# A two-layer streaming encoder step: the MLPs' down projections by seven block products instead of eight, PSUM as four two-bank tiles

## The chip, the cores and the metric

The kernel runs on one core of a Trainium2 chip. The metric is the device time of one execution in microseconds (us), compared by the median over runs. About 0.2% (5 us) is what a measurement of this kernel can tell from no change.

Engine names follow the profile: PE multiplies matrices (PEld is its loading of the stationary operand), DVE is the vector engine, ACT the scalar engine, POOL the GpSimd engine, SP issues most DMA transfers. PSUM is the accumulator memory that PE writes, eight banks of 512 float32 columns on 128 partitions; SBUF is the working memory.

## The reference

One inference step of a trunk with two layers, 1024 features, on 1024 prompt frames and 32 sample frames. Layer 0 mixes tokens with a gated linear recurrence (HGRN2), layer 1 with a gated depthwise convolution of width 3. Both are followed by the same kind of MLP, and a last norm ends the step:

```python
def trunk(x, ...):
    h = x
    for i in range(DEPTH):
        a = rmsnorm(h, norm_mix[i])
        if i % N_MIXERS == 0:
            y, s = hgrn2_mixer(a, ...)
        else:
            y, s = short_conv_mixer(a, ...)
        h = h + y
        m = rmsnorm(h, norm_mlp[i])
        h = h + jnp.square(jax.nn.relu(m @ w_up[i])) @ w_down[i]
    return rmsnorm(h, norm_final), ...
```

`w_up` is 1024 x 4096 and `w_down` 4096 x 1024, so each of the MLP's two products has 1024 x 4096 weights over 1056 tokens. All is float32.

## The kernel before, in words

**Layout.** Activations lie transposed: features on the 128 partitions, the 1056 tokens (prompt and sample together) along the columns. A tensor of 1024 features is eight tiles of 128 x 1056. Tokens are taken in three groups of 384, 384 and 288 (`GROUPS`, L28), each of which fits one PSUM bank.

**Precision.** A float32 operand is used as two float32r parts: a rounded upper part and the remainder. `wsplit` (L94) loads a 512 x 256 block of weights by SP's DMA into `raw`, ACT rounds it into `whi` (L91) and DVE subtracts it into `wlo` (L92). A product is three matmuls (`mm3`, L104): low weights by upper activations, upper by low, upper by upper, accumulated in one bank.

**Order.** The kernel is written as a plain sequence; a planner of the framework orders each engine's instructions ahead of time by their place in the program and by when it thinks their operands and buffers are free. That order is fixed when the kernel runs; each engine takes its queue in order, and semaphores hold an instruction until its operands are there. Weight blocks rotate through four pairs of `whi` and `wlo` buffers and three `raw`, so the loads and splits of the next blocks are interleaved with the work on the current ones. PSUM is two pools of single-bank tiles, three `pj` and five `rc`; `bank()` (L171) takes them in turn. Eighteen long buffers of 128 x 1056 (the pool `fp`, tag `ft`) hold the residual stream `hT` (eight of them) and, in the MLP, the activations.

**The MLP** (`mlp`, L668) goes over the 4096 inner features in eight chunks of 512. Up: for each of the chunk's four column blocks and each token group, 8 row tiles x 3 matmuls into a bank, then DVE applies relu and the norm's factor (L688), ACT squares (L689) and rounds to `uh` (L690), DVE subtracts to `ul` (L691). Down: for each of the eight output blocks and each group, 4 row tiles x 3 matmuls, then DVE adds the bank into `hT` (L698). After the last chunk of the first MLP, `fin0` adds the row's squares into the next norm's sum (`Norm.add`, L623: a square on ACT, a sum on POOL) and splits the row for the convolution (`split`, L175: ACT, then DVE at L182). In the last chunk of the second MLP the down part goes group by group (`FGROUPS`, L29), and the final norm of a finished group (`fin1`) runs among the next group's matmuls. `Norm.scale` (L632) sums the squares over the partitions with three matmuls and works out 1/rms on DVE; the first evictions behind it wait for that factor.

The weights are laid out on the host (`_lay`): `_grid` makes each 512 x 256 block one contiguous piece, four tiles of 128 rows by 256 columns.

Of the kernel before, what the change touches and what calls it, by code (L numbers as in the profile page):

```python
# [8 lines left out]
F32 = mybir.dt.float32  # L9
# [14 lines left out]
FC = 512  # L24
NFC = FF // FC
# [4 lines left out]
# columns of the short vectors  # L30
# [4 lines left out]
def trunk_kernel(  # L35
# [24 lines left out]
    pj = ctx.enter_context(tc.tile_pool(name="pj", bufs=3, space=PSUM))  # L60
    rc = ctx.enter_context(tc.tile_pool(name="rc", bufs=5, space=PSUM))
# [19 lines left out]
    vec = cp.tile([P, NV], F32, name="vec")  # L81

# [41 lines left out]

    def rsqrt(v, y, t):
        """y = 1/sqrt(v) for v > 0: first guess from the exponent bits, three Newton steps."""
# [7 lines left out]
    def tok_rsqrt(pool, accs, n, mid=None):  # L134
        """accs, each [128, n]: squares, still to be summed -> 1/rms per token, [128 tokens, blocks]"""
        nb = -(-n // P)
        ps = pjt()
# [18 lines left out]
    def tok_spread(y, n):  # L156
        """per-token values [128 tokens, blocks] -> the same on every partition, PSUM [128, n]"""
        out = []
        for g0 in range(0, n, 512):
            ps = pjt()  # L160
# [7 lines left out]

    banks = [0]

    def bank():  # L171
        banks[0] += 1
        return pjt() if banks[0] % 8 in (0, 3, 6) else rct()
# [10 lines left out]
    # =============== layer 0, HGRN2 mixer ===============  # L184
# [18 lines left out]
    # masks and the zeroed tiles whose unwritten parts stay zero  # L203
# [9 lines left out]
    # the sample tokens stand twice on the partitions: their values come in two summands (v_sample)  # L213
# [14 lines left out]
    def lower_bounds():  # L228
        """lower bound of the forget gate: first row of the softmax over the two rows"""
# [32 lines left out]
    def gates(H):  # L262
        """decays within blocks of 32, taken from the middle of the block"""
# [22 lines left out]
        # products of whole-block decays, per chunk of four blocks  # L286
# [35 lines left out]
    def carry(H):  # L322
# [6 lines left out]
        # keys decayed to the end, queries from the start, of their half (or quarter) chunk  # L329
# [36 lines left out]
    def o_turn(H, src, nt, nch, col):  # L366
        """normed o back to features on partitions, gained and gated in place of the gate"""
# [8 lines left out]
    def scores(H, half):  # L376
        """within the chunks: decayed keys against queries, masked, and the keys turned"""
# [131 lines left out]
    for pr in range(HEADS // 2):  # L509
# [57 lines left out]
        # the recurrence, step by step between the products of the remaining projections  # L567
# [18 lines left out]
    hp_cm.__exit__(None, None, None)  # L586

    # =============== shared by the rest ===============
    mp = ctx.enter_context(tc.tile_pool(name="mp", bufs=1, reuse_waits="tile"))
    def mm_block(ps, n, c0, wt, j, srcs, kk0=0):  # L590
# [9 lines left out]
    def mm_rows(pss, wt, j, srcs, mid=None):  # L600
        """one block of 128 columns, all token groups, row tile by row tile: uses up the operands in turn"""
# [14 lines left out]
    class Norm:  # L616
        """sum of squares of hT over the features, collected as the rows of hT get final"""
# [14 lines left out]
        def scale(self):  # L632
            v = mp.tile([P, NTOK], F32, tag="sq", name="nv")
            for g in range(3):
                sl, n = gsl(g)
                ps = bank()
# [6 lines left out]
    def out_proj(W, first):  # L643
        """hT += W^T applied to the split activations; ends with the split of the next ones"""
        nrm = Norm()
        for m2 in range(4):
            wt = wload(W, m2)
            for j in range(2):
# [4 lines left out]
                pss = [bank() for g in range(3)]  # L653
# [13 lines left out]

    def mlp(layer, nrm, on_final, last):  # L668
        Wu, Wd = wg_up[layer], wg_down[layer]
        for c in range(NFC):  # L670
            uh = [fp.tile([P, NTOK], F32R, tag="ft", name=f"uh{j}") for j in range(4)]
            ul = [fp.tile([P, NTOK], F32R, tag="ft", name=f"ul{j}") for j in range(4)]
            for m2 in range(2):
                wt = wload(Wu, 2 * c + m2)
                for j in range(2):
                    m = 2 * m2 + j
                    first = c == m == 0
                    pss = [bank() for g in range(3)]
                    if first:
                        mm_rows(pss, wt, j, xsrc, nrm.scale)  # L680
                    for g in range(3):
                        sl, n = gsl(g)
                        ps = pss[g]
                        if not first:
                            mm_block(ps, n, sl.start, wt, j, xsrc)
                        r = nrm.r
                        t = mp.tile([P, 384], F32, tag="t", name="t", bufs=3)
                        nc.vector.scalar_tensor_tensor(t[:, :n], ps[:, :n], 0.0, r[:, sl], op0=ALU.max, op1=ALU.mult)  # L688
                        nc.scalar.activation(t[:, :n], t[:, :n], AF.Square)  # L689
                        nc.scalar.copy(uh[m][:, sl], t[:, :n])  # L690
                        nc.vector.tensor_tensor(ul[m][:, sl], t[:, :n], uh[m][:, sl].bitcast(F32), op=ALU.subtract)  # L691
            usrc = list(zip(uh, ul))

            def down(wt, m, j, c0, n):
                sl = slice(c0, c0 + n)
                ps = bank()
                mm_block(ps, n, sl.start, wt, j, usrc)
                nc.vector.tensor_tensor(hT[m][:, sl], hT[m][:, sl], ps[:, :n], op=ALU.add)  # L698

            dw = lambda m2: [wsplit(Wd[m2, c])]  # L700
            if c == NFC - 1 and last:
                wts = [dw(m2) for m2 in range(4)]
                for g in range(3):
                    for m in range(KT):
                        down(wts[m // 2], m, m % 2, *FGROUPS[g])
                        on_final(g, m)
            else:
                for m2 in range(4):
                    wt = dw(m2)
                    for j in range(2):  # L710
                        for g in range(3):
                            down(wt, 2 * m2 + j, j, *GROUPS[g])
# [192 lines left out]
```

## Time and profile before

| | |
|---|---|
| median of 3 runs | 2498.1 us (2497.3 to 2500.84) |
| span of the profiled execution, first to last instruction | 2495.9 us |
| median less that span | 2.2 us |
| busy PE, DVE, ACT, POOL | 99%, 46%, 24%, 6% of the span |
| mean granted clock of PE | 0.998 |

The span is that of one profiled execution; no other time is given for that execution. A busy share counts the time in which an engine has an instruction running. A row of a group of instructions gives line, engine, operation, output<-inputs, shape and count; after the bar the busy time in us and the mean of one in ns, then how long the engine was idle just before them and what ended that. A row of the timeline gives the start in us, the duration in us, then the instruction; in square brackets the idle time before it and what ended it. Matmuls overlap: each shows its whole latency, so the distance from one start to the next, not the duration, is what one costs. The table of stretches has one row per stretch of the span: length, then busy time of PE, PEld, DVE, ACT and POOL with instruction counts, the granted clock, the DMA engines' share and GB/s.

### The profile page before, as it was taken

Reading aid. Unit: us, or ns where it says so; the run is one execution under the profiler, and the core shown is the slowest. Engines: PE = TensorE matmul, PEld = TensorE weight load, DVE = VectorE, ACT = ScalarE, POOL = GpSimd, SP = SyncE. Lnnn points to the kernel's source line nnn. Section 1 sums busy time; section 2 is a strip of 40 time slices with the busy share of each in tenths; the row PEclk is TensorE's granted clock in tenths of the full one; section 3 lists DMA queues with packets and bytes.
Section 4 is the critical chain, followed back from the end, with each engine's and each line's share of the span. In section 5 each row is a group of like instructions: output and inputs, shape, how many; then the busy total and the mean of one; then the engine's idle time right before and its main releaser. Section 6 shows DMA issues by size and latency. Waiting matters only on the chain.

```text
span 2495.9 us, 36430 instructions
## 1 busy us (share of the span) xinstructions
PE 2474.1 (99%) x15852; PEld 2445.1 (98%) x15852; DVE 1160.3 (46%) x2023; ACT 589.9 (24%) x1020; POOL 159.2 (6%) x328
## 2 busy tenths in 40 slices
PE   8999999999999999999999999999999999999998
PEld 8999999999999999999999999999999999999997
DVE  8775757554533333333336533335533333333335
ACT  5121212133221221221223111123221221221224
POOL 2110101012000000000002000002000000000003
PEclk9999999999999999999999999999999999999999
DMA  4111010121111111111111111111111111111101
GB/s 148 38 32 44 28 48 22 54 106 51 43 43 51 43 43 51 46 39 51 51 35 51 50 35 51 52 34 51 51 35 51 51 34 51 52 36 50 51 26 70
DMA packets 35743, 121.81 MB, mean 49 GB/s; under 512 B 4336, under 2 KB 7552, under 8 KB 35584
## 3 DMA queue, kind: packets, MB, share of 16 engines
q1 hardware_dynamic: 33632, 113.58, 14.0%
q0 software_dynamic: 1952, 5.92, 0.7%
q8 instruction: 124, 2.03, 0.3%
q14 instruction: 35, 0.29, 0.0%
HBM read 114.09 MB, written 5.39 MB: 48 GB/s over the span
## 4 chain that ended last, share of the span: by engine, by line
PE 98%; DVE 1%; ACT 0%; DMA 0%; issue 0%; DVEq 0%; SPq 0%; ACTq 0%
PE rc L105 17%; PE rc L106 16%; PE rc L107 16%; PE pj L105 13%; PE pj L106 13%; PE pj L107 13%; PE v L490 1%; PE v L491 1%; PE v L492 1%; PE aps L383 1%; PE aps L388 1%; PE ops L425 1%; PE ups L400 1%; PE ops L424 1%; PE aps L386 0%; PE kps L393 0%
## 5 line engine op out<-in xcount | busy, mean ns | idle before, releaser
L105 PE MATMUL rc<-xh,wlo 128*128 128x384 f32 (+1 forms) x1600 | 518.9, 325 | 0.0
L106 PE MATMUL rc<-xl,whi 128*128 128x384 f32 (+1 forms) x1600 | 517.2, 323 | 0.0
L107 PE MATMUL rc<-xh,whi 128*128 128x384 f32 (+1 forms) x1600 | 516.7, 323 | 0.0
L105 PE MATMUL pj<-xh,wlo 128*128 128x288 f32 (+1 forms) x1472 | 480.5, 327 | 7.0 <-ACT xh L181 7.0
L106 PE MATMUL pj<-xl,whi 128*128 128x288 f32 (+1 forms) x1472 | 475.2, 323 | 1.9 <-DVE xl L179 1.9
L107 PE MATMUL pj<-xh,whi 128*128 128x288 f32 (+1 forms) x1472 | 474.5, 322 | 0.0
L91 ACT CAST whi<-raw 128x1024 fp32r<-128x1024 f32 (+1 forms) x201 | 209.9, 1046 | 950.5 <-PE rc L107 646.1
L105 PE MATMUL rc<-uh,wlo 128*128 128x288 f32 (+3 forms) x960 | 310.7, 324 | 0.0
L107 PE MATMUL rc<-uh,whi 128*128 128x288 f32 (+3 forms) x960 | 310.0, 323 | 0.0
L106 PE MATMUL rc<-ul,whi 128*128 128x288 f32 (+3 forms) x960 | 310.0, 323 | 0.0
L105 PEld LDWEIGHTS rc<-xh,wlo 128*128 128x128 f32 x1600 | 300.6, 188 | 0.4 <-ACT xh L181 0.2
L106 PEld LDWEIGHTS rc<-xl,whi 128*128 128x128 f32 x1600 | 300.8, 188 | 0.2
L107 PEld LDWEIGHTS rc<-xh,whi 128*128 128x128 f32 x1600 | 300.9, 188 | 0.0
L92 DVE TENSOR_TENSOR wlo<-raw,whi 128x1024 fp32r<-128x1024 f32 (+1 forms) x201 | 244.5, 1219 | 92.7 <-ACT whi L91 92.0
L105 PEld LDWEIGHTS pj<-xh,wlo 128*128 128x128 f32 x1472 | 276.5, 188 | 8.7 <-ACT xh L181 7.0
L106 PEld LDWEIGHTS pj<-xl,whi 128*128 128x128 f32 x1472 | 276.7, 188 | 2.3 <-DVE xl L179 2.3
L107 PEld LDWEIGHTS pj<-xh,whi 128*128 128x128 f32 x1472 | 276.6, 188 | 0.0
L698 DVE TENSOR_TENSOR hT<-hT,rc 128x288 f32<-128x288 f32 (+3 forms) x240 | 124.6, 520 | 251.8 <-PE rc L107 251.7
L689 ACT ACTIVATE t<-t 128x384 f32<-128x384 f32 (+1 forms) x192 | 95.4, 499 | 442.1 <-DVE t L688 440.3
L105 PE MATMUL pj<-uh,wlo 128*128 128x384 f32 (+3 forms) x576 | 186.2, 323 | 0.0
L106 PE MATMUL pj<-ul,whi 128*128 128x384 f32 (+3 forms) x576 | 185.9, 323 | 0.0
L107 PE MATMUL pj<-uh,whi 128*128 128x384 f32 (+3 forms) x576 | 185.7, 322 | 0.0
(214 smaller groups left out, 2916.4 us busy)
## 6 DMA issues: line engine op xcount, KB each, us to landing
raw<-in_wg_up_dram SPq DMA_DIRECT2D x64, 512.0 KB, 3.8
raw<-in_wg_down_dram SPq DMA_DIRECT2D x64, 512.0 KB, 3.2
raw<-in_wg_in_hgrn_dram SPq DMA_DIRECT2D x31, 512.0 KB, 4.0
raw<-in_wg_cu_conv_dram SPq DMA_DIRECT2D x16, 512.0 KB, 3.3
xk<-in_x_t_dram SPq DMA_DIRECT2D x8, 528.0 KB, 8.5
hT<-in_x_t_dram POOLq DMA_DIRECT2D x8, 528.0 KB, 7.2
raw<-in_wg_out_hgrn_dram SPq DMA_DIRECT2D x8, 512.0 KB, 3.9
raw<-in_wg_b_conv_dram SPq DMA_DIRECT2D x8, 512.0 KB, 3.3
```

Source lines behind the costliest of these rows:

```text
L91: nc.scalar.copy(hi, raw)
L92: nc.vector.tensor_tensor(lo, raw, hi.bitcast(F32), op=ALU.subtract)
L105: nc.tensor.matmul(ps, wlo, ah, start=start, stop=False)
L106: nc.tensor.matmul(ps, whi, al, start=False, stop=False)
L107: nc.tensor.matmul(ps, whi, ah, start=False, stop=stop)
L383: nc.tensor.matmul(o, H.K[:, sl], H.F[:, sl], start=True, stop=True)
L388: nc.tensor.matmul(o[0:64, 64:128], kl[:, 64:128], ql[:, 64:128], start=True, stop=True)
L400: nc.tensor.matmul(ups[:, ci * P : (ci + 1) * P], H.kT[half][:, ci], H.V[:, 4 * half + ci], start=True, stop=True)
L424: nc.tensor.matmul(o, H.C[:, c * P : (c + 1) * P], prev, start=True, stop=False)
L425: nc.tensor.matmul(o, at[half][:, ci], H.V[:, c], start=(c == 0), stop=True)
L689: nc.scalar.activation(t[:, :n], t[:, :n], AF.Square)
L698: nc.vector.tensor_tensor(hT[m][:, sl], hT[m][:, sl], ps[:, :n], op=ALU.add)
```

## The change

**Products.** Each MLP's inner features are taken in 16 chunks of 256 instead of 8 of 512. The down product of such a chunk, for each half of the 1024 output features, is cut into 2 x 2 blocks: weights by 128 inner features and 256 output features (two column tiles `p` of 128 to a block), activations by 128 inner features and half of the tokens (528). The block product is formed by seven products of sums of blocks (a form of Strassen's scheme with the sums nested as S1 to S4, T3, T4, Q1, Q2) where the plain form has eight. `STEPS` gives their order and the PSUM tile (`a`, `b` or `c`) each accumulates in: some products add to a tile whose earlier partial sum has already been read out, because that sum is needed in two output blocks. A product is three matmul passes over two token quarters of 264 columns, one per bank of a two-bank tile, and each product is followed by an eviction of 528 columns into `hT`.

**Evictions.** Those of steps 1 to 5 are DVE additions from PSUM. Those of steps 0 and 6 are copies by ACT into one of four `st` tiles and additions by POOL; in the last chunk of the first MLP (`final`) they are DVE additions too.

**Sums of weights** (`wsums`): a block's upper part and remainder are made for three of the four tiles as stored; then POOL forms four sums in place in `raw`, and ACT and DVE split those into a second pair of `whi` and `wlo` buffers. **Sums of activations** (`xsums`): seven operands, each a rounded part by ACT and a remainder by DVE, and four sums by DVE in place.

**Up part.** Two column blocks a chunk. The first two token groups share a two-bank tile and are evicted by one DVE instruction of 768 columns; relu, norm factor and square stay in float32 in the long buffers, the split now belongs to `xsums`.

**Order.** A chunk's up part is emitted, then the down part of the chunk before, then the sums of the chunk's activations. In the second MLP the last two chunks keep the plain product with the final norm among it; their activations are split into the operand tiles `xh`, `xl` that the up part has then done with.

**PSUM.** After the recurrence the two pools are closed, and one pool of four two-bank tiles takes their place. Every block of three groups in the rest of the kernel takes two such tiles (`trio`), and so do the norm's three matmuls; single uses take one (`newps`).

The host's layout of `w_down` changes with it (`_blocks`): the four tiles of a piece are the four blocks.

```diff
+    pb = ctx.enter_context(tc.tile_pool(name="pb", bufs=4, space=PSUM, reuse_waits="tile"))
+    def pt():
+        return pb.tile([P, 2, 512], F32, tag="pb", name="pb")
+    def trio():
+        a, b = pt(), pt()
+        return a, [a[:, 0], a[:, 1], b[:, 0]]
...
+    WAT = {"A11": (0, 0), "A12": (0, 1), "A22": (0, 2), "S2": (1, 0), "S4": (1, 1), "S1": (1, 2), "S3": (1, 3)}
+    STEPS = (("a", "A11", "B11", True), ("b", "S1", "Q1", True), ("a", "S2", "Q2", False), ("b", "S4", "B22", False),
+             ("a", "S3", "T3", False), ("c", "A12", "B21", True), ("a", "A22", "T4", False))
+    def wsums(src):
+        raw, hi, lo = wtiles()
+        hi2 = ws.tile([P, 4, 256], F32R, tag="whi", name="whi")
+        lo2 = ws.tile([P, 4, 256], F32R, tag="wlo", name="wlo")
+        nc.sync.dma_start(out=raw, in_=src)
+        nc.scalar.copy(hi[:, :3], raw[:, :3])
+        nc.vector.tensor_tensor(lo[:, :3], raw[:, :3], hi[:, :3].bitcast(F32), op=ALU.subtract)
+        for d, o in ((2, 3), (3, 0), (0, 2), (1, 0)):
+            nc.gpsimd.tensor_tensor(raw[:, d], raw[:, d], raw[:, o], op=ALU.add)
+        nc.scalar.copy(hi2, raw)
+        nc.vector.tensor_tensor(lo2, raw, hi2.bitcast(F32), op=ALU.subtract)
...
+    def xsums(u0, u1):
+        b11, b12, b21, b22 = u0[:, :HALF], u0[:, HALF:], u1[:, :HALF], u1[:, HALF:]
...
+            t = fp.tile([P, 2, HALF], F32R, tag="ft", name=f)
+            h, l = t[:, 0], t[:, 1]
...
+                nc.scalar.copy(h, src)
+                nc.vector.tensor_tensor(l, src, h.bitcast(F32), op=ALU.subtract)
...
+        part("B11", b11)
+        part("B22", b22)
+        add(b22, b12, b22, ALU.subtract)
+        add(b12, b11, b12, ALU.subtract)
+        add(b11, b22, b11, ALU.subtract)
+        part("Q1", b12)
+        part("Q2", b11)
+        part("T3", b22, True)
+        part("B21", b21)
+        add(b21, b11, b21, ALU.add)
+        part("T4", b21, True)
...
     def mlp(layer, nrm, on_final, last):
...
+                nc.vector.scalar_tensor_tensor(two(u), a[:, :, :384], 0.0, two(r), op0=ALU.max, op1=ALU.mult)
+                sq(u[:, :768])
+                nc.vector.scalar_tensor_tensor(u[:, 768:], pss[2][:, :288], 0.0, r[:, 768:], op0=ALU.max, op1=ALU.mult)
+                sq(u[:, 768:])
...
+        def down(c, final=False):
+            x = X.pop(c)
+            for b in range(2):
+                w = wsums(Wd[c, b])
+                ps = [{}, {}]
+                for i, (bank, f, g, start) in enumerate(STEPS):
+                    for p in range(2):
+                        if start:
+                            ps[p][bank] = pt()
+                        t = ps[p][bank]
+                        (hi, lo), (xhi, xlo) = w(f, p), x[g]
+                        for n, (wf, xf) in enumerate(((lo, xhi), (hi, xlo), (hi, xhi))):
+                            for q in range(2):
+                                nc.tensor.matmul(t[:, q, :QT], wf, xf[:, q * QT : (q + 1) * QT],
+                                                 start=start and n == 0, stop=n == 2, skip_group_check=True)
...
+                        if i in (0, 6):
+                            d, op = (C(0, 0), ALU.add) if i == 0 else (C(1, 0), ALU.subtract)
+                            if final:
+                                acc(d, op)
+                            else:
+                                st = mp.tile([P, HALF], F32, tag="st", name="st", bufs=4)
+                                nc.scalar.copy(q2(st), v)
+                                nc.gpsimd.tensor_tensor(d, d, st, op=op)
+                        elif i == 1:
+                            acc(C(1, 1), ALU.subtract)
+                        elif i == 2:
+                            acc(C(0, 1), ALU.add)
+                        elif i == 3:
+                            acc(C(0, 1), ALU.add)
+                        elif i == 4:
+                            acc(C(1, 1), ALU.subtract)
+                        else:
+                            acc(C(0, 0), ALU.add)
+                if final:
+                    for m in range(4 * b, 4 * b + 4):
+                        on_final(m)
+        if not last:
+            for c in range(NFC):
+                up(c)
+                if c:
+                    down(c - 1)
+                sums(c)
+            down(NFC - 1, True)
+            return
+        n = NFC - 2
+        for c in range(n):
+            up(c)
+            if c:
+                down(c - 1)
+            sums(c)
+        up(n)
+        up(n + 1)
+        for k in range(4):
+            split(k, U[n + k // 2][k % 2])
+        down(n - 1)
...
```

More of the change, by code (lines that the diff above doesn't have):

```diff
@@ L652, in out_proj @@
                     nc.gpsimd.dma_start(out=hT[m], in_=x_t[m * P : (m + 1) * P, :])
-                pss = [bank() for g in range(3)]
+                _, pss = trio()
                 if m in (0, KT - 1):
@@ L668, in mlp @@
     def mlp(layer, nrm, on_final, last):
         Wu, Wd = wg_up[layer], wg_down[layer]
[L670 to L680, printed above, removed]
+        U, X = {}, {}
@@ L692, in mlp @@
[L692 to L712, printed above, removed]
-                        if c == NFC - 1:
-                            on_final(2 * m2 + j)
@@ L716, in trunk_kernel @@
-    for k in range(KT):
-        split(k, heads[k].Y)
+                        mm_block(pss[g], n, sl.start, wt, j, xsrc)
+                r = nrm.r
+                spare = last and (c, j) == (NFC - 1, 1)
+                u = mp.tile([P, NTOK], F32, tag="sq", name="ulast") if spare else ft("u")
+                nc.vector.scalar_tensor_tensor(two(u), a[:, :, :384], 0.0, two(r), op0=ALU.max, op1=ALU.mult)
+                sq(u[:, :768])
+                nc.vector.scalar_tensor_tensor(u[:, 768:], pss[2][:, :288], 0.0, r[:, 768:], op0=ALU.max, op1=ALU.mult)
@@ L744, in trunk_kernel @@
                                       vec[:, V_SC : V_SC + 16].rearrange("p (j m) -> p m j", m=KT)[:, m])
[L745 removed]
+                _, pss = trio()
                 if m == 0:
@@ L778, in trunk_kernel @@
             for j in range(2):
-                pss = [bank() for g in range(3)]
+                _, pss = trio()
                 last = 2 * m2 + j == KT - 1
```

104 lines of the change are left out of this document (79 added, 25 removed).

## The prediction

> **What bounds the kernel now.** I read the page first: busy time, granted clock, chain of waits.
>
> ```profile
> span 2495.9 us, 36430 instructions
> PE 2474.1 (99%) x15852; PEld 2445.1 (98%) x15852; DVE 1160.3 (46%) x2023; ACT 589.9 (24%) x1020; POOL 159.2 (6%) x328
> ...
> PEclk9999999999999999999999999999999999999999
> ...
> PE 98%; DVE 1%; ACT 0%; DMA 0%; issue 0%; DVEq 0%; SPq 0%; ACTq 0%
> ```
>
> PE is 98% of the chain at full clock. The table of stretches shows that in the first MLP it never idles:
>
> ```profile
> 672.00:1443.00 771.00, 771.00 (x4786) 770.37 (x4785) 311.72 (x477) 171.38 (x253) 20.79 (x17) 1.00 0.14 46
> ```
>
> DVE works 40% of that stretch, ACT 22%, POOL 3%, DMA 14%. So the number of matmul columns sets the time, and removing some pays in full as long as no other engine takes PE's place. The pitches come first. In the timeline of DVE a block of 36 matmuls (4 row tiles, 3 passes, 384+384+288 columns) ends once per three additions:
>
> ```profile
> 1222.82 0.56 DVE L698 TENSOR_TENSOR hT<-hT,rc 128x384 f32<-128x384 f32 x1 [1.07 <-PE rc L107]
> 1224.41 0.45 DVE L698 TENSOR_TENSOR hT<-hT,rc 128x288 f32<-128x288 f32 x1 [1.04 <-PE rc L107]
> ...
> 1257.66 0.56 DVE L698 TENSOR_TENSOR hT<-hT,pj 128x384 f32<-128x384 f32 x1 [1.44 <-PE pj L107]
> ```
>
> The second group of the first block ends at 1222.82 and that of the seventh at 1257.66: (1257.66 - 1222.82)/6 = 5.807 us a block. The third group's 12 matmuls of 288 columns take 1.59 us, 0.1325 each. Matmuls of 256 columns, each with its own weight load, in PE's timeline, 20 pitches apart:
>
> ```profile
> 59.83 0.28 PE L491 MATMUL v<-wlo,xh 128*128 128x256 f32 x1
> ...
> 62.17 0.28 PE L504 MATMUL v<-whi,xsm 128*64 128x256 f32 x1
> ```
>
> That is 2.34/20 = 0.117 us.
>
> **The change: what PE saves.** No row has 264 columns; the two rows are 0.457 and 0.460 ns a column, so it lies between them at 0.117 + 8/32 x 0.0155 = 0.1209 us (bounds 0.117 and 0.1325). A down chunk of 256 rows has 2 halves of the output x 7 products x 2 column tiles x 3 passes x 2 banks = 168 matmuls, 20.3 us. Before, 512 rows took 8 blocks, 46.45 us, so 256 rows 23.2. Saved: 2.92 us a chunk, for 16 chunks in the first MLP and 14 in the second (its last two stay as they were): **-87.5 us** (at the two bounds, -106 and -28; proportional rows leave some 4 us either way of them).
>
> [...]
>
> **What the other engines get.** Durations by form, from the groups:
>
> ```profile
> L698 DVE TENSOR_TENSOR hT<-hT,rc 128x384 f32<-128x384 f32 x155 | 85.7, 553 | 175.5 <-PE rc L107 175.4
> L698 DVE TENSOR_TENSOR hT<-hT,rc 128x288 f32<-128x288 f32 x75 | 34.0, 454 | 73.6 <-PE rc L107 73.6
> L283 DVE TENSOR_TENSOR R<-R,ab 128x528 f32<-128x528 f32 x8 | 5.6, 701 | 0.0
> L92 DVE TENSOR_TENSOR wlo<-raw,whi 128x1024 fp32r<-128x1024 f32 x199 | 243.1, 1224 | 92.3 <-ACT whi L91 91.6 <-issue 0.3
> L91 ACT CAST whi<-raw 128x1024 fp32r<-128x1024 f32 x199 | 208.7, 1050 | 949.0 <-PE rc L107 646.1 <-PE pj L107 296.4 <-DMA raw<-in_wg_in_hgrn_dram 4.3
> L395 ACT COPY kT<-kps 128x512 f32<-128x512 f32 x16 | 9.4, 587 | 128.6 <-PE kps L393 128.6
> L629 POOL TENSOR_TENSOR acc<-acc,sq 128x1056 f32<-128x1056 f32 x21 | 54.0, 2572 | 265.0 <-ACT sq L628 265.0
> L838 POOL TENSOR_TENSOR hT<-hT,fr 128x416 f32<-128x416 f32 x8 | 9.4, 1204 | 719.7 <-ACT fr L834 719.7
> L838 POOL TENSOR_TENSOR o<-hT,fr 128x256 f32<-128x256 f32 x2 | 1.8, 938 | 3.9 <-ACT fr L834 3.9
> ```
>
> A DVE addition of 528 columns out of PSUM is 0.553 + 144 x 0.00103 = 0.70 us, as the 528-wide row; POOL's of 528, between 416 and 1056 columns, 1.44; ACT's copy of 528 about 0.60. A chunk's up and down take PE 4 x 5.807 + 20.3 = 43.5 us. In it:
> - DVE: 20 additions 14.0; the up part's evictions, two of 768 and two of 288 columns, 2.8; remainders of the up weights 2 x 1.22, of the down weights and their sums 2 x (0.92 + 1.22); 11 operations on sums of activations 7.7. Together 31.2 us.
> - POOL: 8 sums of weights at 0.94 and 8 additions at 1.44: 19.0 us.
> - ACT: roundings 2.1 + 3.7, squares 2.5, 7 parts and 8 copies at 0.60: 17.3 us.
>
> SP's queue issues as many blocks of 512 KB as before. Each engine fits under PE's 43.5 us, so the average costs nothing; the crowding inside the down part does.
>
> **A down half, steps 1 to 5.** A product of one column tile is 6 matmuls, 0.725 us, and ends in one 528-column eviction. In steps 1 to 5 of 7 these are DVE's, 0.70 us each and some 0.03 between: DVE runs level with PE, and anything else put there makes it late. A tile is written again three products after its last matmul, 2.18 us. How soon an eviction starts:
>
> ```profile
> 1203.59 0.29 PE L105 MATMUL rc<-xh,wlo 128*128 128x288 f32 x1
> ...
> 1203.79 0.56 DVE L688 SCALAR_TENSOR_TENSOR t<-pj,nr 128x384 f32<-128x384 f32 x1 [1.96 <-PE pj L107]
> ```
>
> PE was in the next block at 1203.59, DVE began at 1203.79: 0.20 us. So 2.18 - 0.20 - 0.70 = 1.28 us of lateness is free; beyond it the matmul that accumulates into, or takes over, the tile waits, and with it all of PE's queue. In steps 6 and 0 ACT and POOL evict, and DVE has 10.15 - 7.3 = 2.85 us. Per half 4.13 us of other work go in.
>
> Half 0 has the next half's two remainders, 2.14 us, hidden even when each is held up as below. Half 1 has those of the next up weights, 2.44, whose buffers only half 0 frees, and what falls there of the 11 operations on sums. Also POOL, busy 4 x 1.44 = 5.8 of 10.15 us there, holds up DVE operations that read two operands from SBUF, as at the end of the trace (POOL, then DVE):
>
> ```profile
> 2458.06 9.35 POOL L838 TENSOR_TENSOR hT<-hT,fr 128x416 f32<-128x416 f32 x8 [719.68 <-ACT fr L834]
> ...
> 2459.25 0.55 DVE L698 TENSOR_TENSOR hT<-hT,rc 128x384 f32<-128x384 f32 x1 [1.74 <-PE rc L107]
> 2460.40 1.24 DVE L809 TENSOR_TENSOR facc<-facc,fsq 128x384 f32<-128x384 f32 x1 [0.59 <-ACT fsq L807]
> 2461.56 0.54 DVE L698 TENSOR_TENSOR hT<-hT,pj 128x384 f32<-128x384 f32 x1
> 2462.70 1.37 DVE L809 TENSOR_TENSOR facc<-facc,fsq 128x384 f32<-128x384 f32 x1 [0.59 <-ACT fsq L807]
> ...
> 2467.53 0.56 DVE L809 TENSOR_TENSOR facc<-facc,fsq 128x384 f32<-128x384 f32 x1 [0.59 <-ACT fsq L807]
> ```
>
> L809 reads two SBUF tiles: 0.56 us alone, 1.24 and 1.37 beside POOL, so 0.75 more; L698, with one operand in PSUM, is untouched. With one operation on sums in half 1, and POOL met 5.8/10.15 = 0.57 of the time, 0.43 us an operation, the load is 2.44 + 0.70 + 3 x 0.43 = 4.4 us, 0.3 over; with two, 2.44 + 1.40 + 4 x 0.43 = 5.55, 1.4 over. With none it fits; with all eleven it is 2.44 + 7.7 + 13 x 0.43 = 15.7, 11.6 over. I take one to two, 0.9 us: the 18 long buffers hold 8 rows of the residual, 7 operand tiles and 2 new activations, which leaves one, so the next operands can only be written as the old ones end, step by step through half 1, and most land in the next up part, where DVE is nearly free. For 28 chunks (15 and 13, the layer ends apart): **+25 us**, bounds 0 and 325.
>
> The weights' own chain is rounding 0.80, remainder 0.92, four POOL sums 3.76, rounding 1.05, remainder 1.22: 7.75 us, and 10.6 with two POOL additions of 1.44 queued ahead. Half 1's second product, the first that needs a sum, starts 10.15 + 1.45 = 11.6 us after the buffers come free: hidden by 1.0 us; each further POOL addition ahead would cost some 0.4 a chunk. POOL's additions of step 0 are done 5.8 us later, before DVE adds to the same rows at step 5 (7.25).
>
> **Once per layer.** The last chunk of the first MLP evicts everything on DVE, 14 x 0.73 = 10.2 of 10.15 us a half, and its half 1 also gets the splits of rows 0 to 3. Such splits, the sum of squares beside them, and the chain to the convolution's first eviction, before:
>
> ```profile
> 1359.93 2.52 POOL L629 TENSOR_TENSOR acc<-acc,sq 128x1056 f32<-128x1056 f32 x1 [3.36 <-ACT sq L628]
> ...
> 1360.95 2.62 DVE L182 SCALAR_TENSOR_TENSOR xl<-hT,vec,xh 128x1056 fp32r<-128x1056 f32 x1 [0.83 <-ACT xh L181]
> ...
> 1368.62 0.56 DVE L638 TENSOR_SCALAR nv<-rc 128x384 f32<-128x384 f32 x1 [5.05 <-PE rc L637]
> ...
> 1384.69 0.51 DVE L758 TENSOR_TENSOR z<-pj,r 128x256 f32<-128x256 f32 x2
> ```
>
> Four splits of 1.25 (by DVE's slope) to 2.6 us less the 1.28 give 4 to 9: I take 5. Then rows 4 to 7 end together. Before, they came 5.8 us apart; now four squares (about 1.05 by the 1024-wide row) and four POOL sums of 2.5 follow each other through one buffer, 14.2 us, and 1384.69 - 1368.62 = 16.1 us more until a tile comes free: 30 us. Four two-bank tiles hold two blocks, 23.2 us and the norm's three matmuls, where eight banks held 31. Stall 5, bounds 0 and 7. After the two output projections one row is late, not four; there the norm's matmuls stand behind seven of eight row tiles, 10.2 + 16.1 = 26.3 us: 1 each (0 to 3). Before the last Strassen chunk of the second MLP four splits of 1.25 us stand ahead of the evictions on DVE: 5.0 - 1.28, some 4 (0 to 5). Together **+16 us**, bounds 4 and 27.
>
> Sum: -87.5 + 25 + 16 = -46.5. Against the span of 2495.9 that is 2449.4; what lies around it I take as the median's 2.2 us over the span. Forecast **2452 us**.
>
> **The rivals.**
> 1. All hidden: the planner puts every filler into steps 6 and 0. Then -87.5 + 4 to 16, 2415 to 2427 us. For it: the average loads of 72%, 40% and 44%. Against it: DVE at 0.73 per 0.725 us in steps 1 to 5.
> 2. Slower: POOL and DVE in turns within half 1. If five operations on sums are ordered into it, the load is 2.44 + 3.5 + 7 x 0.43 = 8.95, 4.8 us over; 28 x 4.8 = 135, giving 2498 - 87.5 + 135 + 16 = 2562. It decides from (87.5 - 16)/28 = 2.55 us a chunk, which three such operations just reach; four, 3.7 us over, give 2530. For it: the held-up rows, and that an order fixed ahead doesn't know of them. Against it: the one spare buffer.
> 3. DVE becomes the bound of whole chunks: all 17 operations with two SBUF operands held up by 0.75, 31.2 + 12.8 + 41 x 0.03 = 45.2 us a chunk against the 46.4 of before: 28 x -1.2 - 6 + 16 = -24, 2474 us, and up to 2490 as its load isn't even. [...] Against it: POOL is busy only 44% of a chunk.
> 4. The products don't get cheaper, because a wait at every change of tile breaks PE's stream: from 0.1 us at each of 28 changes the saving of 2.9 us is gone, 2498 + 16 = 2514. Against it: in the stretch quoted PE changes banks every 12 matmuls and never idles.
>
> **How the numbers follow.** Forecast, 2430 to 2470: 0.45; all hidden: 0.27; slower in half 1: 0.15; DVE the bound: 0.09; no cheaper: 0.04. The range from 2412 to 2508 leaves out a little below the first rival and most of the second; the likeliest's own is 2430 to 2470. What a measurement here can tell from no change is about 0.2%, 5 us: faster than 2493 takes the forecast, rival 1 and four fifths of rival 3, 0.79; same 0.05; slower 0.16.
>
> **What would show it.** In the stretch of the first MLP PE's busy share falls below 100%, and the matmuls of 264 columns follow at 0.121 us. In the waits, PE waits for DVE's additions into hT, near 25 us in total, and hardly for ACT's copies; near 1310 to 1350 us the seam to the convolution shows PE idle for some 5 us. DVE remainders of 528 columns last 0.70 alone and up to 1.5 beside POOL. It would be wrong if PE waited for POOL's additions or the weight sums (a product whose summed weights come late), if the pitch weren't proportional to the columns, or if most operations on sums stood between the evictions.

## The result, and the profile after

The changed kernel takes 2513.45 us (median of 4 runs, 2513.28 to 2513.47); the kernel before, run beside it, 2499.47 us. The ratio is 1.0057, 95% interval 1.0043 to 1.0071: **slower by 14 us**, where 46 us faster was forecast. The profiled execution has a span of 2511.6 us, 15.7 more than before.

The page of the changed kernel: span, busy shares, granted clock, chain of waits.

```profile
span 2511.6 us, 39447 instructions
...
PE 2424.9 (97%) x16572; PEld 2383.0 (95%) x16572; DVE 1617.9 (64%) x2409; ACT 776.4 (31%) x1270; POOL 773.7 (31%) x800
...
PEclk9999999999999999999998999999999999999999
...
PE 82%; DVE 8%; POOL 5%; ACT 3%; issue 2%; DMA 0%; DVEq 0%; SPq 0%; ACTq 0%; POOLq 0%
```

PE has 16 points less of the chain than before (98%): DVE, POOL and ACT now stand in it. Stretches of the changed kernel (length; busy PE, PEld, DVE, ACT, POOL; granted clock; DMA share; GB/s):

```profile
672.00:1300.00 628.00, 615.92 (x4376) 612.95 (x4375) 453.48 (x576) 230.47 (x350) 293.70 (x225) 1.00 0.15 48
1300.00:1345.00 45.00, 34.13 (x260) 33.09 (x258) 40.52 (x53) 19.41 (x26) 26.10 (x22) 0.95 0.07 24
1345.00:1360.00 15.00, 8.82 (x50) 8.85 (x51) 12.30 (x13) 4.01 (x5) 7.33 (x4) 0.59 0.31 105
...
1385.00:1405.00 20.00, 13.25 (x71) 12.94 (x70) 13.73 (x17) 2.92 (x3) 0.47 (x4) 0.83 0.00 1
```

In the steady part of the first MLP PE idles 2% of the time; at its end and at the start of the convolution it idles up to four tenths of it, and then its clock is low as well. What PE waited for, in us, times and the longest:

```profile
PE pb L794 <- DVE hT L800: 25.0, 29, 0.9
PE pb L794 <- DVE wlo L712: 17.3, 2, 11.2
PE pb L108 <- DVE z L898: 6.8, 1, 6.8
...
PE pb L108 <- DVE u L772: 4.3, 2, 2.1
PE pb L656 <- POOL acc L647: 4.1, 1, 4.1
```

To see which stage lost what, the three norms whose squares PE sums with a matrix of ones cut the span in four. PE's timeline, the first such matmul of each, before:

```profile
624.25 1.13 PE L637 MATMUL rc<-acc,ones 128*128 128x384 f32 x3
...
1367.78 0.48 PE L637 MATMUL rc<-acc,ones 128*128 128x384 f32 x1
...
1741.40 0.48 PE L637 MATMUL rc<-acc,ones 128*128 128x384 f32 x1
```

and after:

```profile
629.93 0.81 PE L656 MATMUL pb<-acc,ones 128*128 128x384 f32 x2
...
1378.19 1.01 PE L656 MATMUL pb<-acc,ones 128*128 128x384 f32 x1 [4.14 <-POOL acc L647]
...
1766.12 0.48 PE L656 MATMUL pb<-acc,ones 128*128 128x384 f32 x1
```

The four lengths are the differences of these starts, the last one up to the end of the span. The columns on the right are the same for the experiments below.

| stage, us | before | after | remainder later | and one bank | and plain ends |
|---|---|---|---|---|---|
| mixer 0 and its output projection | 624.2 | 629.9 | 630.2 | 625.7 | 623.7 |
| MLP 1 | 743.5 | 748.3 | 731.5 | 732.3 | 716.1 |
| convolution and its output projection | 373.6 | 387.9 | 388.5 | 375.4 | 373.6 |
| MLP 2 to the end | 754.5 | 745.5 | 729.6 | 728.6 | 722.8 |
| span | 2495.9 | 2511.6 | 2479.8 | 2461.9 | 2436.3 |

MLP 1 gained nothing at all, and 20 us were lost in stages that hold no Strassen product.

### The profile page after: what moved, and what is told of

It is laid out like the page before. It is cut to its first block, busy times and chain, and to the rows that moved or that the text cites. A ratio compares the mean times of both kernels' runs of the same rounds, so it can differ in the third digit from the quotient of the medians.

```text
span 2511.6 us, 39447 instructions
## 1 busy us (share of the span) xinstructions
PE 2424.9 (97%) x16572; PEld 2383.0 (95%) x16572; DVE 1617.9 (64%) x2409; ACT 776.4 (31%) x1270; POOL 773.7 (31%) x800
## 3 DMA queue, kind: packets, MB, share of 16 engines
q0 software_dynamic: 1952, 5.92, 0.7%
## 4 chain that ended last, share of the span: by engine, by line
PE 82%; DVE 8%; POOL 5%; ACT 3%; issue 2%; DMA 0%; DVEq 0%; SPq 0%; ACTq 0%; POOLq 0%
PE pb L794 17%; PE pb L108 15%; PE pb L109 15%; PE pb L110 15%; POOL raw L710 4%; PE pj L108 4%; PE pj L109 3%; PE pj L110 3%; DVE wlo L712 1%; DVE hT L800 1%; PE v L493 1%; PE v L492 1%; ACT whi L711 1%; PE v L494 1%; DVE wlo L708 1%
## 5 line engine op out<-in xcount | busy, mean ns | idle before, releaser
L108 PE MATMUL pb<-xh,wlo 128*128 128x384 f32 (+3 forms) x2592 | 847.6, 327 | 11.8 <-DVE z L898 6.8
L109 PE MATMUL pb<-xl,whi 128*128 128x384 f32 (+3 forms) x2592 | 839.4, 324 | 0.7 <-DVE xl L184 0.7
L110 PE MATMUL pb<-xh,whi 128*128 128x384 f32 (+3 forms) x2592 | 839.9, 324 | 0.0
L108 PEld LDWEIGHTS pb<-xh,wlo 128*128 128x128 f32 x2592 | 489.0, 189 | 17.4 <-DVE z L898 7.8
L109 PEld LDWEIGHTS pb<-xl,whi 128*128 128x128 f32 x2592 | 489.4, 189 | 1.3 <-DVE xl L184 1.0
L110 PEld LDWEIGHTS pb<-xh,whi 128*128 128x128 f32 x2592 | 488.8, 189 | 0.5
L808 POOL TENSOR_TENSOR hT<-hT,st 128x528 f32<-128x528 f32 x232 | 404.7, 1771 | 249.1 <-ACT st L807 249.1
L800 DVE TENSOR_TENSOR hT<-hT,pb 128x528 f32<-128x528 f32 x608 | 392.3, 694 | 48.2 <-PE pb L794 43.9
L710 POOL TENSOR_TENSOR raw<-raw 128x256 f32<-128x256 f32 x240 | 211.4, 881 | 540.7 <-DVE wlo L708 526.8
L794 PE MATMUL pb<-B,whi 128*128 128x264 f32 x1440 | 233.8, 284 | 0.0
L712 DVE TENSOR_TENSOR wlo<-raw,whi 128x1024 fp32r<-128x1024 f32 x60 | 75.4, 1257 | 111.2 <-ACT whi L711 111.2
```

The costliest lines, as they stand in the source:

```text
L108: nc.tensor.matmul(ps, wlo, ah, start=start, stop=False)
L109: nc.tensor.matmul(ps, whi, al, start=False, stop=False)
L110: nc.tensor.matmul(ps, whi, ah, start=False, stop=stop)
L710: nc.gpsimd.tensor_tensor(raw[:, d], raw[:, d], raw[:, o], op=ALU.add)
L712: nc.vector.tensor_tensor(lo2, raw, hi2.bitcast(F32), op=ALU.subtract)
L794: nc.tensor.matmul(t[:, q, :QT], wf, xf[:, q * QT : (q + 1) * QT], start=start and n == 0, stop=n == 2, skip_group_check=True)
```

## The experiments

The kernel before, run beside each group, was 2500.7 to 2500.9 us in the median; ratios are against it.

**What stalls the steady part.** One chunk of the changed kernel, in the timeline: DVE, ACT, POOL and PE rows of the first half of a down part, by time of start.

```profile
762.30 3.18 POOL L710 TENSOR_TENSOR raw<-raw 128x256 f32<-128x256 f32 x4 [15.76 <-DVE wlo L708]
...
765.51 1.05 ACT L711 CAST whi<-raw 128x1024 fp32r<-128x1024 f32 x1 [1.50 <-POOL raw L710]
...
766.59 1.26 DVE L712 TENSOR_TENSOR wlo<-raw,whi 128x1024 fp32r<-128x1024 f32 x1 [1.10 <-ACT whi L711]
...
767.03 0.65 PE L794 MATMUL pb<-B,whi 128*128 128x264 f32 x4
...
767.78 4.99 DVE L800 TENSOR_TENSOR hT<-hT,pb 128x528 f32<-128x528 f32 x8
...
768.52 0.51 PE L794 MATMUL pb<-T,wlo 128*128 128x264 f32 x2 [0.84 <-DVE hT L800]
```

DVE's queue has the second remainder (L712, of the summed weights of half 1) ahead of the additions of step 2. Its operand comes through POOL's sums and ACT's rounding, so DVE stands idle for 1.10 us with additions ready behind it, then works 1.26 us on the remainder. The additions are 2.36 us late, 1.28 us of that is free, and PE loses the rest at step 4: 1.49 us from the row at 767.03 to that at 768.52 where four matmuls take 0.49. Three runs test this.

*e2: the same remainder, behind the additions of step 3.* The edit:

```diff
+        with tc.issue_after(after) if after else ExitStack():
+            nc.vector.tensor_tensor(lo2, raw, hi2.bitcast(F32), op=ALU.subtract)
...
+                        if (i, p) == (3, 1) and b == 0:
+                            late = e.ins
```

`late` is the last addition of step 3 in half 0; the weight sums of half 1 get it as `after`.

> One edit to the changed kernel: in every down part DVE's remainder of the second half's summed weights is queued behind its addition of step 3, second column tile, of the first half; before, it stood between the additions of steps 1 and 2, where DVE waited 1.1 us for ACT's rounding, which waited for POOL's sums. Theory 'late sums': PE's wait of about 1 us in each of 28 down parts (29 us in all) is that wait in DVE's queue; it goes, and the chunk's period falls from 44.8 to 43.7 us, the time by 25 to 30 us, to some 2485. Rival 'crowding' (the prediction's): DVE has no room in steps 1 to 5, so the 1.26 us of the remainder delay the later additions instead, PE waits about 1 us at step 5 or 6, and the time changes by under 5 us.

Measured: **2481.6 us** (2480.22 to 2481.81), ratio 0.9923 [0.9906, 0.9939], 32 us under the changed kernel. The stretch of the first MLP, DVE's queue at the same place, and the first and a late row of PE in that down part:

```profile
672.00:1300.00 628.00, 628.00 (x4506) 628.00 (x4505) 471.61 (x594) 236.74 (x360) 297.48 (x235) 1.00 0.15 49
```

```profile
759.65 0.40 PE L796 MATMUL pb<-B,wlo 128*128 128x264 f32 x2
...
762.05 4.37 DVE L802 TENSOR_TENSOR hT<-hT,pb 128x528 f32<-128x528 f32 x6 [1.47 <-PE pb L796]
766.34 1.22 DVE L713 TENSOR_TENSOR wlo<-raw,whi 128x1024 fp32r<-128x1024 f32 x1
...
779.61 0.65 PE L796 MATMUL pb<-T,whi 128*128 128x264 f32 x4
```

No idle time is left in front of the remainder, and PE is busy all 628 us. The 164 matmuls from 759.65 to 779.61 take 0.1217 us each.

*e3: no sums on POOL.* The loop of four `nc.gpsimd.tensor_tensor` additions (L709, L710) is left out, so that the second set of weights of each half goes in unsummed.

> The changed kernel without POOL's four sums of weight tiles in each half of a down part; the second roundings and remainders are made of the weights as stored, so four of the seven products take the wrong weights. Theory 'late sums': without POOL in that chain the remainder is ready 3 us sooner, the wait of 1 us in each of 28 down parts goes and the period falls from 44.8 to about 43.7 us; the waits of 11.2 and 6.1 us at the ends of the MLPs shrink as well; time about 2465 to 2485. Rival 'crowding': DVE's own work is what it was, the wait stays at 0.5 to 1 us a chunk, time above 2490.

Measured: 2482.1 us (one run). PE in the same stretch:

```profile
672.00:1300.00 628.00, 627.85 (x4473) 624.91 (x4473) 461.43 (x588) 234.56 (x360) 183.20 (x116) 1.00 0.15 49
```

With the operand early the remainder may stay where it is. e2 and e3 change different things and reach the same time: the steady stall was the late sums together with DVE's fixed order. At the end of MLP 1 nothing is gained by it: PE's wait for the summed weights falls from 11.2 to 0.7 us there, but waits for DVE's additions (4.7 and 1.7), for the parts of the activations (3.6) and for ACT's squares (3.5) come in its place, and the stage takes 734.1 us, 2.6 more than in e2.

*e8: no additions by POOL.* The additions of steps 0 and 6 on POOL (L808) are left out; the output lacks those products. This asks whether POOL's additions, running beside DVE's operations, are what makes DVE late.

> The changed kernel without GpSimd's additions of the first and last product into hT (its output lacks those two products of every block but the last chunk's; the weight sums on GpSimd stay). Theory 'late sums': GpSimd had been idle for 15.76 us when the sums of half 1's weights came to it, so its additions are not in that chain, and the wait of 1.04 us in each chunk stays: period 44.8 us, time within 4 us of 2513.5. Rival 'GpSimd holds up VectorE' (the forecast's term of 0.75 us per sum): VectorE's remainders and sums run undisturbed, the wait falls by half or more and the time by 12 to 25 us.

Measured: 2506.3 us (one run), 3 us under what the first theory allowed and 5 above the rival's. A group of DVE, changed kernel:

```profile
L708 DVE TENSOR_TENSOR wlo<-raw,whi 128x768 fp32r<-128x768 f32 x60 | 86.6, 1443 | 30.4 <-ACT whi L707 30.4
```

and without POOL's additions, with PE's wait:

```profile
L708 DVE TENSOR_TENSOR wlo<-raw,whi 128x768 fp32r<-128x768 f32 x60 | 57.2, 954 | 30.3 <-ACT whi L707 30.3
```

```profile
PE pb L794 <- DVE hT L800: 24.1, 30, 0.9
```

POOL's additions do stretch these remainders (1.44 us against 0.95), but PE's wait for the additions is unchanged, 24.1 against 25.0 us: the stretched operations lie where DVE has time. The chunks of the stretch are as long as before; the 7 us came outside them, at the two MLPs' ends (by the norms' matmuls MLP 1 is 2.2 and MLP 2 5.1 us shorter).

**The end of MLP 1.** In the changed kernel's last chunk DVE, POOL and PE show this (by time of start):

```profile
1331.66 5.61 DVE L800 TENSOR_TENSOR hT<-hT,pb 128x528 f32<-128x528 f32 x9
...
1337.20 0.94 DVE L708 TENSOR_TENSOR wlo<-raw,whi 128x768 fp32r<-128x768 f32 x1
...
1339.93 2.41 POOL L647 TENSOR_TENSOR acc<-acc,sq 128x1056 f32<-128x1056 f32 x1
1342.30 5.28 POOL L710 TENSOR_TENSOR raw<-raw 128x256 f32<-128x256 f32 x3
...
1351.18 0.78 PE L794 MATMUL pb<-Q,wlo 128*128 128x264 f32 x2 [11.20 <-DVE wlo L712]
```

The weights' chain of half 1 starts behind nine additions in a row, and its sums on POOL share the engine with the next norm's squares and take 1.76 us each (5.28/3) where the four of the steady chunk above take 0.80 (3.18/4); PE waits 11.20 us for the summed weights.

*e1: both halves' weight sums written ahead of the last chunk's products.*

```diff
+            ws2 = [wsums(Wd[c, b]) for b in range(2)] if final else None
-                w = wsums(Wd[c, b])
+                w = ws2[b] if final else wsums(Wd[c, b])
```

> One edit to the changed kernel: in the last chunk of the first MLP the weights of both output halves, with their sums, are emitted ahead of the products, so that the squares and splits of the first half's finished rows no longer stand before them on ACT, POOL and DVE. Theory 'order': PE's wait of 11.2 us for DVE's second remainder (at 1340 us) and the slow clock behind it are that queue, so the wait falls under 2 us and the time falls by 12 to 18 us, from 2513 to some 2498. Rival 'too much work there': DVE and POOL have more work in that half than PE whatever the order (14 additions, four splits, four sums of squares, the weight sums), so PE waits as long for DVE's additions or splits instead, and the time changes by under 4 us.

Measured: 2515.9 us, ratio 1.0063 [1.0048, 1.0078]: no gain, so the rival held. The one long wait became several:

```profile
1326.88 2.13 PE L795 MATMUL pb<-Q,whi 128*128 128x264 f32 x8 [3.42 <-DVE Q L734]
...
1350.77 0.81 PE L795 MATMUL pb<-B,wlo 128*128 128x264 f32 x2 [3.64 <-DVE hT L801]
```

Moving the sums alone is not enough: DVE has the parts of the activations, the remainders, 28 additions and the splits of four rows to do in that chunk.

**The stages without Strassen products.** *e4: the kernel before with PSUM as four two-bank tiles, and nothing else.* In the diff: the closing of `pj` and `rc` after the recurrence, `pt()` and `trio()`, and `trio()` in place of `bank()`.

> The kernel before with only the change of PSUM: four two-bank tiles after the recurrence, every block of three groups taking two of them, down products as before. It prices the PSUM part alone. Theory 'fewer tiles cost the seams': two blocks in flight instead of 2.7, so PE waits some 2 us at the start of each MLP and 3 to 7 us at the convolution, with the slow clock behind each wait, and some us where the recurrence's pools close: 8 to 18 us slower than before. Rival 'PSUM is free': the seams after the change are slow because of the four rows that end together and of DVE's load, and this kernel is within 3 us of the kernel before.

Measured: **2554.8 us**, ratio 1.0217 [1.0202, 1.0233]. The PSUM part alone costs 54 us, several times what was expected. The norms' matmuls:

```profile
630.25 0.81 PE L653 MATMUL pb<-acc,ones 128*128 128x384 f32 x2
...
1393.22 0.48 PE L653 MATMUL pb<-acc,ones 128*128 128x384 f32 x1
...
1780.51 0.48 PE L653 MATMUL pb<-acc,ones 128*128 128x384 f32 x1
```

By stage that is +6.0, +19.4, +13.7 and +17.7 us. The first and third are what the changed kernel lost there (+5.7, +14.3). Three mechanisms are in the trace; no run takes them apart. First, in each block (PE, and the DVE row it follows):

```profile
1022.81 0.56 DVE L704 SCALAR_TENSOR_TENSOR t<-pb,nr 128x384 f32<-128x384 f32 x1 [2.32 <-PE pb L109]
...
1023.27 0.29 PE L109 MATMUL pb<-xh,whi 128*128 128x288 f32 x1
1023.43 0.44 PE L107 MATMUL pb<-xh,wlo 128*128 128x384 f32 x1
1023.71 0.34 PE L108 MATMUL pb<-xl,whi 128*128 128x384 f32 x1
```

The first two token groups are the two banks of one tile, so the second group's first matmul waits until DVE has read the first group: it starts at 1023.43, 0.06 us after DVE's end at 1023.37, and 0.28 us pass to the next matmul in place of 0.176, (5.807 - 1.59)/24 by the forecast's rows. Six matmuls of the third group are put in between, and still 0.10 us is lost; by the distances from start to start there are eleven such losses, 1.31 us together, in the chunk from 1000.0 to 1094.1 us. Second, at a norm: the three matmuls of `Norm.scale` take a pair of tiles of their own, so PE stops after one more block: it waits 5.65 us for the first evictions at each MLP's start and 6.75 at the convolution, where the kernel before has no such wait. Third, where the recurrence ends, the output projection has no PSUM until the old pools are closed: PE waits 4.35 us for DVE's part of the last head, while the kernel before runs the projection's matmuls there. *e7* ran the same program again:

> The kernel before with PSUM as four two-bank tiles, once more, for a second profile: MLP 1 between its norm and the convolution's again near 763 us, the convolution near 387 us. If the first matmul of a block again takes 0.10 us longer than the others the loss belongs to the program, if not to the one execution.

Measured: 2554.8 us and a span of 2552.8 us, the same to 0.1 us; the loss belongs to the program.

*e5: e2, and eight single banks outside the Strassen parts.* `pj` and `rc` stay open up to the first up part of MLP 1, then two-bank tiles, then eight single banks after the last Strassen chunk:

```diff
+                else:
+                    two_banks()
...
             down(NFC - 1, True)
+            one_bank()
```

`two_banks` and `one_bank` close the open pools and open the next; the first stands after the first up part.

> The changed kernel with the second remainder of half 1 held back as in the run that gave 2481.6 us, and PSUM in eight single banks outside the Strassen parts: the recurrence's two pools stay open through the output projection and the first up part of MLP 1, the four two-bank tiles are opened after it and closed after the last Strassen chunk, and the convolution, its output projection, the first up part of MLP 2 and the plain chunks use eight single banks. Theory 'too few blocks in flight': with four two-bank tiles two blocks of three token groups fill PSUM, so TensorE stops wherever the vectors are late by more than a block; with eight banks the seam from the recurrence loses its 5.9 us, the convolution its 14 us, and each MLP's start 2.3 us or more: 25 to 28 us less than 2481.6, so 2453 to 2457, the convolution back at 374 us between its two norms. Rival 'the seams pay for the four rows at a time': the waits are for hT rows that the Strassen scheme finishes four at a time, so the convolution keeps more than 10 of its 14 us and the time stays above 2468.

Measured: **2462.0 us** (2461.55 to 2463.67), ratio 0.9846 [0.9829, 0.9864], 19.6 us under e2: between the theory's 25 and the rival's 14.

```profile
625.66 0.81 PE L674 MATMUL rc<-acc,ones 128*128 128x384 f32 x2
...
1357.92 1.01 PE L674 MATMUL sb<-acc,ones 128*128 128x384 f32 x1 [3.25 <-POOL acc L665]
...
1733.31 0.48 PE L674 MATMUL sb<-acc,ones 128*128 128x384 f32 x1
```

The convolution has 13.1 of its 14.9 us back and the recurrence's seam 4.5, so the rival falls. One run undoes all three mechanisms here, so their shares stay open. What did not come back are the MLPs' starts, where PE still waits for the first evictions, now before it may enter the two-bank tiles:

```profile
PE pb L108 <- DVE u L794: 4.2, 2, 3.0
```

*e6: e5, and plain ends.* MLP 1's last two chunks by eight products as MLP 2 has them, and the four splits of the plain chunks' operands spread over half 1 of the last Strassen chunk:

```diff
+                    if b and i in (0, 2, 4, 5) and parts:
+                        k = parts.pop(0)
+                        split(k + k0, U[NFC - 2 + k // 2][k % 2])
...
-        for k in range(4):
-            split(k, U[n + k // 2][k % 2])
-        down(n - 1)
+        down(n - 1, [0, 1, 2, 3])
```

Both layers now take this way. In MLP 1 both changes act at once, in MLP 2 only the second; the convolution's operands of rows 4 to 7 are split behind the last row.

> The kernel with single banks at the seams, and besides the last two chunks of MLP 1 by eight products (rows final one after the other, as MLP 2 has them), and in both MLPs the four splits of the plain chunks' operands spread over half 1 of the last Strassen chunk instead of ahead of it. Theory 'the last chunk's own chain': MLP 1's end loses some 21 us to waits for the sums and remainders of one chunk that nothing covers, and MLP 2's last Strassen chunk 8 us; plain products cost 2 x 2.92 = 5.8 us more: 20 us less than the kernel with single banks at the seams, within 5. Rival 'the work only moves': VectorE and ScalarE have the same splits, remainders and squares to do at that place whatever their order, as it was when both halves' weight sums were emitted first; then the gain is under 6 us.

Measured: **2438.0 us** (2436.31 to 2438.52), ratio 0.9749 [0.9732, 0.9767], 24.0 us under e5 and 63 under the kernel before: as fast as any run here.

```profile
623.72 0.48 PE L674 MATMUL rc<-acc,ones 128*128 128x384 f32 x1
...
1339.86 0.48 PE L674 MATMUL sb<-acc,ones 128*128 128x384 f32 x1
...
1713.47 0.48 PE L674 MATMUL sb<-acc,ones 128*128 128x384 f32 x1
```

MLP 1 is 16.1 us shorter and MLP 2 5.8, although 28 chunks instead of 30 have the cheaper products. The wait for POOL's sum of squares at the convolution's norm is gone too.

*e9: e6 with the two-bank tiles opened after the second up part.*

> The kernel with plain ends, and in each MLP the two-bank tiles are opened after the second up part instead of the first. There the trace has TensorE idle for 3.1 and 2.7 us, until VectorE has scaled the first blocks with the norm. Theory 'two-bank tiles wait for all banks they overlap at the start': with single banks the second chunk's up part begins at once, 4 to 6 us less than 2438.0. Rival 'the norm itself is late': the wait goes to another block and at most 1 us is gained.

Measured: 2437.8 us (2434.3 to 2438.35). Nothing is gained; in MLP 1 the wait went to the first down part:

```profile
671.13 0.51 PE L820 MATMUL pb<-Q,wlo 128*128 128x264 f32 x2 [2.23 <-ACT st L830]
```

At this place the rival held: DVE and ACT are late behind the norm, wherever the tiles open.

## Why the prediction was wrong, step by step

- **PE's saving, -87.5: right but for the size.** The pitch at 264 columns is 0.1217 us, not 0.1209, so a chunk takes 20.45 us and saves 2.78: 30 x 2.78 = 83.4.
- **DVE as a sum, 72% of a chunk: right** (453.48 of 628 us). So the rival in which DVE bounds whole chunks falls, and with it the one where half 1 is slower; PE's wait comes once a chunk, at step 4 of half 0 (28 of the 29 times).
- **Steady stalls, +25: the size near, the place wrong.** PE's wait for the additions is 25.0 us, the very number forecast, but in half 0; that the numbers agree is luck. The step that failed is "Half 0 has the next half's two remainders, 2.14 us, hidden even when each is held up". It counted the remainders as work and not as waits: in DVE's queue the remainder whose operand was late (1.10 us of idle time) held up the additions behind it. The slack of 1.28 us was right: 1.10 + 1.26 - 1.28 = 1.08 where PE lost about 1.0. In time it is the 32 us that e2 took away, 1.14 a chunk for 28 chunks. Half 1's crowding did not come: "0.70 us each and some 0.03 between" is wrong in its sign, since eight additions in a row take 4.99 us, (4.99 - 0.694)/7 = 0.614 from start to start.
- **"Hidden by 1.0 us", the weights' own chain:** held for PE in every steady chunk, and failed where DVE and POOL had the layer's end to do as well: 11.2 and 6.1 us (the 17.3 in two waits). A product whose summed weights come late is one of the signs that the prediction itself named for being wrong.
- **Once per layer, +16: the step that decided the sign.** Measured it is 15.7 + 83.4 - 32 = 67 us. By stage, with the saving of 16 and 14 chunks and the steady stalls of 15 and 13 taken out: mixer 0 5.7, MLP 1 32, convolution 14.3, MLP 2 15. Of the forecast's terms, "5 last chunk" met the wait of 11.20 us, smaller ones before it, and a slow clock (0.50) behind it; "5 seam to convolution" met 4.14 for the sum of squares and 6.75 for the first eviction, since "Four two-bank tiles hold two blocks ... and the norm's three matmuls" is false: the norm's matmuls take one of the two pairs, and behind them PE has the last row of one block and two groups of the next, from 1380.18 to 1390.48, before it waits. "1 each" was 2.1 and 2.1 (4.3 in two waits), inside its bounds. "4 before the last Strassen chunk of the second MLP" was 6.1 in one wait alone, above its bound of 5.
- **Left out of the sum:** the recurrence's seam, where the closed pools keep the output projection's first matmuls from running while the last heads are normed (from 520 to 525 us PE is busy 1.70 us, before 3.39); the wait between two banks of one tile (0.10 us in e4); and the clock (0.50 behind the waits of 11.20 and 6.75 us). e4 shows that the PSUM part has its own price, 54 us on the old kernel; the forecast priced it at the seams only, with 5 + 2 us.
- **The rival at 2514 us** gave the measured time within 1 us by luck, with a mechanism that the runs refute: the products did get cheaper, all of it, once the stalls were gone (e2). A time that fits is no evidence for its mechanism. Its condition, a wait at a change of tile that costs 0.1 us, does occur, but in the blocks with an eviction for each bank, not in the Strassen part.

What stays open: the sizes of the pieces within MLP 1's 32 us were not taken apart one by one. PE's waits outside the steady part add up to 23.2 us there (2.14 at the start; 0.98, 2.04, 1.96, 11.20, 0.73 and 4.14 at the end), with the slow clock on top (0.69 from 1328 to 1331 us, 0.50 behind the 11.20 and the 4.14); e6 shows that replacing the last chunks and spreading the splits brings 16 of them back, net of 5.6 us more of matmuls.

## What to carry to other kernels

Before costing an instruction as hidden by its length, look at when its operand arrives and what stands behind it in the same queue; moving one remainder by a few places was worth 32 us here. A change of tile shape for one stage is a change in every stage that uses the pool, so run it alone on the old kernel and look at the seams. With work that nothing covers (the last chunk before a norm) the plain form can be cheaper than the one with fewer products; here that was shown together with the spread splits.

## What the runs showed of the hardware

The clock after an idle time, in PE's stretches of the changed kernel (columns as above), behind the wait of 11.20 us that ended at 1351.18:

```profile
1351.20:1352.70 1.50, 1.50 (x7) 1.50 (x8) 0.66 (x1) 1.50 (x2) 1.50 (x1) 0.50 0.42 82
1352.70:1355.00 2.30, 2.30 (x12) 2.30 (x12) 2.30 (x2) 0.26 (x1) 0.90 (x1) 0.50 0.44 175
1355.00:1357.50 2.50, 2.50 (x14) 2.50 (x13) 2.50 (x4) 0.00 (x0) 0.00 (x0) 0.57 0.66 215
1357.50:1360.00 2.50, 2.50 (x23) 2.50 (x22) 2.50 (x5) 0.00 (x1) 0.00 (x0) 1.00 0.55 205
```

PE runs at half clock for some 6 us (1.50 + 2.30, and 0.86 of the third row by its mean of 0.57). A matmul of 264 columns then takes 0.22 us from start to start (four from 1353.08 to 1353.96) and not 0.1217, 1.8 times as long: the 26 from 1351.18 to 1357.10 take 5.92 us in place of 3.16, another 2.8 us. Behind the wait of 6.75 us the granted clock is 0.50 as well (1397.2 to 1401.0 us), and the slow starts last 4.3 us, from 1397.23 to 1401.55. Waits of up to 0.9 us, as in the steady part, leave the clock at 1.00 (672 to 1300 us).

Not expected: that DVE's additions out of PSUM overlap by 0.08 us (0.614 from start to start, each 0.694 long), and that GpSimd's additions, which lengthen DVE's remainders of 768 columns (L708) by half (0.95 to 1.44 us), leave PE's waits for DVE's additions as they are (25.0 us with them, 24.1 without).
